# A two-layer hybrid attention backbone on one core: shared weights in the output projection, and other orders of projections

## The chip, the cores and the metric

The kernel runs on one core of one Trainium2 chip. The metric is the device time of one execution in microseconds; the time shown for a kernel is the median of its runs. A profiled execution of the same kernel gives the trace, whose times count from the first instruction of the program.

## The reference: what is computed

512 latent tokens and 256 context tokens, all of width 1024, pass two layers in float32. In each layer the rows are RMS-normalised and modulated (scale and shift from a conditioning vector), and one wide input projection feeds three token mixers: multi-head latent attention (MLA), differential attention, and windowed attention with sinks. Each mixer's output is gated by a SiLU path and projected; the three are merged by sigmoid gates and go through one output projection, whose result is gated and added to the rows. Only layer 0 also updates the context tokens.

```python
h_lat = rms_norm(x, norm_g) * (1.0 + scale) + shift
h_ctx = rms_norm(ctx, norm_g) * (1.0 + scale_c) + shift_c
...
terms.append(jax.nn.sigmoid(gr) * ((y * jax.nn.silu(zr)) @ w_branch[r]))
return (terms[0] + terms[1] + terms[2]) @ w_out
...
x = x + gate * merge_branches((ya_l, yb_l, yc_l), z_l, gm_l, w_branch, w_out)
if need_ctx:
    ctx = ctx + gate_c * merge_branches((ya_c, yb_c, yc_c), z_c, gm_c, w_branch, w_out)
```

The last step is an RMS norm of the latent tokens.

## The kernel before, in words

**Tokens and passes.** The 768 tokens are six tiles of 128: tiles 0 and 1 are context, 2 to 5 latent. A float32 product is made of three matmuls on rounded operands: every activation and every weight is split into a high part (rounded by ACT) and a low part (the rest, subtracted by DVE), and the passes are high-high, high-low and low-high. So one contraction block of 128 costs three matmuls. Projections produce feature-major results with the weights as the stationary operand; the output projection produces token-major results with the tokens as the stationary operand and the weights moving, up to 512 columns wide.

**Weights.** All weights come through one stream (`weight_stream`, L392). An item is 128x1024 numbers, 512 KB: `loader` (L397) issues its load on SP into one of two staging buffers (`ws`), and `splitter` (L409) makes its high and low halves in a ring of six buffers (`wh`), so three items are split at a time. A buffer comes free when the last matmul that reads it is done.

**The order of the work.** A planner (`Plan`, L128 on) writes the program: it keeps a modelled time for PE and for every other engine, and emits an instruction when its modelled inputs are ready. What it emits is in order on each engine; on the chip the engines then wait for each other through semaphores. PE is fed from three sources, chosen in `run` (L195): single pieces that became ready (transposes, the modulation's matmuls) go first; stream a holds the attention units in the order windowed, differential, MLA; stream b holds everything else as a list of entries in order (`stream_b`, L1209), at most `DEPTH` = 2 of them in flight, and serves as filler between softmax chains. An entry waits until its slots (46 buffers of 128x768), its gate and its first weight item are ready. The order of stream b is written by hand in two tables. `SEQ` (L45) orders the first projections of each layer: `K` and `Q` and `V` are keys, queries and values of windowed attention, `k`, `q`, `v` of the differential one, `c`, `cn`, `cr` and `p` MLA's queries (latent, norm, rotated part, plain part), `l`, `ln`, `lr`, `u`, `w` its keys and values, and `z20` to `z15` gate projections done early. `BR` (L30) orders the gate projections (`z`), merge gates (`g`) and branch projections (`b`) of the three branches, windowed first. A gate projection waits for all of its mixer's outputs. The constants of the planner's model are in `dma_t` (L334), `score` (L785) and `mod_entry` (L1621).

**The output projection** stands at the end of a layer. `load_res` (L1777) loads the residual rows and the gate vectors. `out_entry` (L1800) makes one block of columns for a set of token tiles: per contraction block it issues three matmuls per tile, and after the eighth it evicts (`chain`): DVE multiplies by the gate and adds the rows, ACT squares for the next norm. The block that ends at column 1024 is the final one: there, for layer 0, a latent tile's new rows are stored to DRAM (`x1_d`, L1850) for layer 1's residual, and `norm_rows` (L661) scales the rows in place, which has to wait until the store has read them. In layer 0 the latent tiles run three blocks (512, 256 and 256 columns) over eight weight items, and then the context tiles two blocks of 512 over the same weights, loaded and split again as eight more items. Between the two stands `next_h` (L1866), which allocates layer 1's inputs and starts `make_group` (L711): it transposes the normalised rows on PE (`make_h`, L671) once all four latent tiles are normalised, modulates each feature block on ACT or DVE and splits it. Layer 1's first projections need these blocks one after the other.

```python
        wide_ = [(0, 512), (512, 512)]
        for c, (a, n) in enumerate([(0, 512), (512, 256), (768, 256)]):
            out_entry(range(2, 6), 0, c, a, n, not cx)
        if cx:
            entry(next_h, need=16)
            for c, (a, n) in enumerate(wide_):
                out_entry(range(2), 1, c, a, n, True)
```

PSUM has four single banks (`bk`) and two double ones (`wd`); the latent tiles' sums and the context's lie in `bk`, the transposes' results in `wd`.

Of the kernel before, what the change touches and what calls it, by code (L numbers as in the profile page):

```python
# [24 lines left out]
D = 1024  # L25
# [4 lines left out]
BR = [['z7 z1 z2 g4 z4 z0 z3 g3 z5 z6 g0 b0 g1 b1 g2 b2 b4 g5 b5 b3 g6 b6 g7 b7', 'z7 z5 z0 z1 z6 z2 z3 g0 z4 g1 g2 g3 b3 b1 g4 b2 b0 b4 g5 g6 b5 g7 b6 b7', 'z7 z2 z6 z3 z1 z5 z4 g0 z0 g2 g1 g3 g4 g5 b1 g6 g7 b0 b3 b2 b4 b5 b6 b7'], ['g0 z4 z3 z0 z5 z7 z2 z1 z6 b0 g1 g5 b1 g2 b2 g3 g4 b3 b4 g6 g7 b6 b5 b7', 'z0 z5 z2 z1 g2 z4 z6 z7 g0 g1 z3 b0 g4 b1 g3 b4 g5 b5 b3 g6 b6 b2 g7 b7', 'z1 z4 z0 z2 z5 g0 z7 z6 g2 z3 g1 g5 g3 g4 g6 g7 b1 b2 b3 b4 b5 b0 b6 b7']]  # L30
# [14 lines left out]
SEQ = ["K0 V Q0 Q1 c0 c1 c2 cn Q2 cr p0 p1 Q3 p2 p3 z20 Q4 K1 z21 Q5 z22 Q6 z23 Q7 v0 k0 q0 z24 k1 q1 v1 k2 q2 l0 l1 ln lr k3 q3 v2 k4 q4 k5 q5 v3 k6 q6 k7 q7 u0 w0 z10 z11 u1 w1 z12 z13 u2 w2 z14 z15 u3 w3",  # L45
       "K0 V Q0 Q1 c0 c1 c2 cn Q2 cr p0 p1 Q3 p2 p3 z20 Q4 K1 z21 Q5 z22 Q6 z23 Q7 v0 k0 q0 z24 k1 q1 v1 k2 q2 l0 l1 ln lr k3 q3 v2 k4 q4 k5 q5 v3 k6 q6 k7 q7 u0 w0 z10 z11 u1 w1 z12 z13 u2 w2 z14 z15 u3 w3"]
# [189 lines left out]
def hybrid_kernel(tc, x_in, c_in, ctx_in, c_ctx, w_mod, b_mod, norm_g, w_in, q_norm, w_uq, kv_norm, w_ukv,  # L236
# [97 lines left out]
    def dma_t(nbytes):  # L334
        P.free["Q"] = max(P.free["Q"], P.now) + 620.0
        t = max(P.free["D"], P.free["Q"] + 650.0) + nbytes / 350.0
        P.free["D"] = t
        return t + 1050.0
# [446 lines left out]
    def score(row, kgroups, maps):  # L785
# [9 lines left out]
        P.tick(0.0 if maps == 1 else 300.0)  # L795
# [491 lines left out]
    def build_layer(o):  # L1287
# [333 lines left out]
        def mod_entry(ll, n, j):  # L1621
            def h():
# [7 lines left out]
                def chain():  # L1630
# [5 lines left out]
                    te = yield from P.pe(lambda: max(t, bk.gate() if j == 0 else 0.0), 750.0, emit)  # L1636
# [140 lines left out]
        def load_res(toks, j):  # L1777
# [3 lines left out]
            def chain():  # L1781
# [5 lines left out]
                G[j] = yield from tmps(2)  # L1787
                for h in range(2):
                    t = max(t, dma(G[j][h][0], gate_d[l][j, h * 512:(h + 1) * 512].partition_broadcast(128)))
# [4 lines left out]
                o.rest[j].t = t  # L1794
# [3 lines left out]
        o.rest = [When(), When()]  # L1798

        def out_entry(toks, j, c, a0, n, last):  # L1800
# [5 lines left out]
            if final and j == 0:  # L1806
                steps = [(tk, k) for tk in toks for k in range(8)]

            def release():
                yield o.rest[j]  # L1810
                for _, rg in G[j]:
                    rg.t = P.now + 3000.0
# [144 lines left out]
```

## Time and profile before

| | us |
|---|---|
| median of 3 runs (lowest to highest) | 2715.02 (2711.09 to 2715.76) |
| the profiled execution's own time | 2711.5 |
| its span, first to last instruction | 2709.7 |
| PE busy | 2632.3 |
| DVE busy | 1615.4 |
| ACT busy | 1350.7 |

The profiled execution's span and its time differ by what lies around the program. A busy PE is not PE at its peak: matmuls are pipelined, so the mean duration of a single one is longer than its share of the time, and a price per matmul is the busy time of a dense group over its count. The granted clock of TensorE has two levels, 1.2 and 2.4 GHz; the column PEclk is their mean over a stretch, as a share of the higher.

### The profile page before, as it was taken

Reading aid. Unit: us, or ns where it says so; the run is one execution under the profiler, and the core shown is the slowest. Engines: PE = TensorE matmul, PEld = TensorE weight load, DVE = VectorE, ACT = ScalarE, POOL = GpSimd, SP = SyncE. Lnnn points to the kernel's source line nnn. Section 1 sums busy time; section 2 is a strip of 40 time slices with the busy share of each in tenths; the row PEclk is TensorE's granted clock in tenths of the full one; section 3 lists DMA queues with packets and bytes.
Section 4 is the critical chain, followed back from the end, with each engine's and each line's share of the span. In section 5 each row is a group of like instructions: output and inputs, shape, how many; then the busy total and the mean of one; then the engine's idle time right before and its main releaser. Section 6 shows DMA issues by size and latency. Waiting matters only on the chain. (4 is left out here: it accounts for less than half of the span.)

```text
span 2709.7 us, 42486 instructions
## 1 busy us (share of the span) xinstructions
PE 2632.3 (97%) x16551; PEld 2291.5 (85%) x16551; DVE 1615.4 (60%) x3010; ACT 1350.7 (50%) x2685; POOL 179.3 (7%) x371
## 2 busy tenths in 40 slices
PE   7999999999999999999999998999999999999998
PEld 5888898888888888888888887898888788888887
DVE  4677887666676652142424577887667676534435
ACT  5676775545665551121222366777546565422333
POOL 2101111111100000000000011111101100000000
PEclk8999999999999999999999999999999999999999
DMA  7133211111132463442322533312111223443433
GB/s 237 47 96 85 66 43 48 53 51 42 49 85 85 140 201 117 121 133 63 103 69 64 186 97 91 85 51 65 55 50 38 72 75 98 122 140 101 131 94 133
DMA packets 332318, 249.55 MB, mean 92 GB/s; under 512 B 24870, under 2 KB 296324, under 8 KB 332116
## 3 DMA queue, kind: packets, MB, share of 16 engines
q1 hardware_dynamic: 331472, 246.50, 31.2%
q8 instruction: 130, 2.13, 0.3%
q0 software_dynamic: 416, 0.30, 0.1%
q14 instruction: 72, 0.59, 0.1%
q10 hardware_dynamic: 228, 0.03, 0.0%
HBM read 211.37 MB, written 35.41 MB: 91 GB/s over the span
## 5 line engine op out<-in xcount | busy, mean ns | idle before, releaser
L444 PE MATMUL wd<-s,wh 128*128 128x512 f32 (+1 forms) x4392 | 852.2, 355 | 2.0 <-DVE s L330 1.5
L444 PEld LDWEIGHTS wd<-s,wh 128*128 128x128 f32 x4392 | 723.7, 189 | 123.1 <-issue 6.7
L444 PE MATMUL bk<-s,wh 128*128 128x512 f32 (+1 forms) x3666 | 763.4, 355 | 8.0 <-DVE s L323 1.8
L444 PEld LDWEIGHTS bk<-s,wh 128*128 128x128 f32 x3666 | 584.2, 190 | 94.9 <-issue 6.8
L323 DVE TENSOR_TENSOR wh<-ws,wh 128x1024 fp32r<-128x1024 f32 (+4 forms) x294 | 324.3, 1108 | 522.5 <-ACT wh L309 520.2
L309 ACT ACTIVATE wh<-ws 128x1024 fp32r<-128x1024 f32 (+4 forms) x294 | 282.9, 967 | 537.7 <-PE wd L444 396.4
L309 ACT ACTIVATE pt<-bk 128x512 fp32r<-128x512 f32 (+3 forms) x604 | 342.2, 583 | 204.8 <-PE bk L914 143.3
L444 PE MATMUL bk<-wh,s 128*128 128x256 f32 (+1 forms) x2400 | 351.3, 300 | 3.9 <-DVE pt L323 3.0
L444 PEld LDWEIGHTS bk<-wh,s 128*128 128x128 f32 x2400 | 319.0, 192 | 19.8 <-DVE pt L323 3.7
L323 DVE TENSOR_TENSOR pt<-bk,pt 128x512 fp32r<-128x512 f32 (+5 forms) x428 | 273.3, 656 | 89.7 <-ACT pt L309 69.8
L444 PE MATMUL bk<-pt,s 128*128 128x256 f32 x1888 | 282.7, 289 | 16.2 <-DVE pt L323 10.6
L444 PEld LDWEIGHTS bk<-pt,s 128*128 128x128 f32 x1888 | 252.5, 192 | 41.0 <-DVE pt L323 19.4
L444 PE MATMUL wd<-s,s 128*128 128x256 f32 (+5 forms) x1872 | 274.3, 332 | 10.2 <-ACT s L309 7.4
L309 ACT ACTIVATE s<-wd,ti 128x768 f32<-128x768 f32 (+1 forms) x240 | 195.3, 817 | 137.7 <-DVE ti L826 79.8
L444 PEld LDWEIGHTS wd<-s,s 64*128 64x128 f32 (+2 forms) x1872 | 210.3, 190 | 38.8 <-ACT s L309 11.9
L914 PE MATMUL bk<-ident,s 128*128 128x128 f32 x1472 | 213.0, 278 | 7.9 <-DVE ti L866 3.0
L914 PEld LDWEIGHTS bk<-ident,s 128*128 128x128 f32 x1472 | 173.3, 143 | 34.5 <-ACT s L309 6.1
L309 ACT ACTIVATE s<-s,ti 128x513 f32<-128x513 f32 (+6 forms) x256 | 183.1, 722 | 26.6 <-DVE ti L862 11.0
L309 ACT ACTIVATE s<-bk 128x256 fp32r<-128x256 f32 (+5 forms) x291 | 113.1, 424 | 77.8 <-PE bk L444 76.5
L826 DVE TENSOR_REDUCE ti<-wd 128x1 f32<-128x768 f32 (+1 forms) x160 | 129.3, 845 | 26.0 <-PE wd L444 25.7
L309 ACT ACTIVATE yo<-bk 128x256 f32<-128x256 f32 (+1 forms) x200 | 72.2, 382 | 141.3 <-PE bk L444 140.1
L862 DVE CUSTOM_DVE_ANT_0 s<-wd,s,sinkt 128x512 f32<-128x512 f32 (+2 forms) x160 | 116.3, 743 | 42.1 <-PE wd L444 41.9
(104 smaller groups left out, 1557.1 us busy)
## 6 DMA issues: line engine op xcount, KB each, us to landing
ws<-in_w_in_dram SPq DMA_DIRECT2D x180, 512.0 KB
ws<-in_w_branch_dram SPq DMA_DIRECT2D x48, 512.0 KB
s<-in_w_mod_dram SPq DMA_DIRECT2D x48, 256.0 KB
s<-in_w_mod_dram SPq DMA_DIRECT2D x32, 384.0 KB
ws<-in_w_out_dram SPq DMA_DIRECT2D x24, 512.0 KB
y<-yo SPq DMA_DIRECT2D x80, 128.0 KB
s<-y SPq DMA_DIRECT2D x24, 384.0 KB
s<-s SPq DMA_DIRECT2D x22, 384.0 KB
```

The costliest lines, as they stand in the source:

```text
L309: lambda: nc.scalar.activation(out=out, in_=in_, func=func, scale=scale, **kw))
L323: t = yield from dve(ready, lambda: nc.vector.tensor_tensor(out=out, in0=a, in1=b, op=op), n)
L444: nc.tensor.matmul(o, lhsT=l, rhs=r, start=first, stop=last)
L826: t = yield from dve(t, lambda: nc.vector.tensor_reduce(out=nmx, in_=p[:, lo:hi], axis=AX.X, op=ALU.max, negate=True), n)
L862: t = yield from dve(t, lambda: nc.vector.tensor_tensor_reduce(out=pt_[:, 0:n], in0=p[:, lo:hi], in1=mk, scale=1.0, scalar=sk, op0=ALU.add ...
L914: nc.tensor.transpose(out=pp[:, j * 256 + ri2 * 128:j * 256 + ri2 * 128 + 128], in_=row["P"][:, c:c + 128], identity=ident)
```

## The change

In layer 0 the output projection takes all six token tiles through the same three column blocks (512, 256, 256), so each weight item is loaded and split once and used by all six. The context tiles' sums move into the two halves of a `wd` pair. `next_h` moves in the list from behind the latent tiles' last block to ahead of the last block, which in token order ends with the two context tiles. Residual rows and gates of all six tiles are loaded in one entry. `SEQ` and `BR` list the same entries in other orders, and four constants of the planner's model change. Layer 1 has no context update; its output projection stays as it was.

```diff
-BR = [['z7 z1 z2 g4 z4 z0 z3 g3 z5 z6 g0 b0 g1 b1 g2 b2 b4 g5 b5 b3 g6 b6 g7 b7', 'z7 z5 z0 z1 z6 z2 z3 g0 z4 g1 g2 g3 b3 b1 g4 b2 b0 b4 g5 g6 b5 g7 b6 b7', 'z7 z2 z6 z3 z1 z5 z4 g0 z0 g2 g1 g3 g4 g5 b1 g6 g7 b0 b3 b2 b4 b5 b6 b7'], ['g0 z4 z3 z0 z5 z7 z2 z1 z6 b0 g1 g5 b1 g2 b2 g3 g4 b3 b4 g6 g7 b6 b5 b7', 'z0 z5 z2 z1 g2 z4 z6 z7 g0 g1 z3 b0 g4 b1 g3 b4 g5 b5 b3 g6 b6 b2 g7 b7', 'z1 z4 z0 z2 z5 g0 z7 z6 g2 z3 g1 g5 g3 g4 g6 g7 b1 b2 b3 b4 b5 b0 b6 b7']]
+BR = [["z7 z4 z2 z1 g4 z0 g2 z3 g0 z5 z6 g3 b4 b2 b0 g1 b3 g6 b1 g5 b5 g7 b6 b7",
+       "z7 z0 z3 z5 z1 z6 z4 g1 g2 g0 z2 g3 b1 g5 b3 b2 g4 b4 g6 b5 b0 g7 b6 b7",
+       "z6 z7 z1 z2 z3 z0 z4 g5 g2 g1 g3 z5 g6 g0 g4 b1 b0 b4 g7 b3 b7 b2 b6 b5"],
+      ["z0 z3 g0 z7 z4 z5 z2 z6 g2 z1 g5 b0 b2 g1 g4 g3 b3 b1 b4 g6 g7 b6 b5 b7",
+       "z7 z0 z5 z2 g0 g2 z4 z1 z3 g1 z6 g4 b1 g3 b0 b4 g5 g6 b3 b5 b6 g7 b2 b7",
+       "z4 z0 z7 z1 z2 z6 g0 z3 z5 g2 g1 g3 g6 g4 g5 b1 b3 b2 b4 g7 b0 b5 b6 b7"]]
...
-SEQ = ["K0 V Q0 Q1 c0 c1 c2 cn Q2 cr p0 p1 Q3 p2 p3 z20 Q4 K1 z21 Q5 z22 Q6 z23 Q7 v0 k0 q0 z24 k1 q1 v1 k2 q2 l0 l1 ln lr k3 q3 v2 k4 q4 k5 q5 v3 k6 q6 k7 q7 u0 w0 z10 z11 u1 w1 z12 z13 u2 w2 z14 z15 u3 w3",
-       "K0 V Q0 Q1 c0 c1 c2 cn Q2 cr p0 p1 Q3 p2 p3 z20 Q4 K1 z21 Q5 z22 Q6 z23 Q7 v0 k0 q0 z24 k1 q1 v1 k2 q2 l0 l1 ln lr k3 q3 v2 k4 q4 k5 q5 v3 k6 q6 k7 q7 u0 w0 z10 z11 u1 w1 z12 z13 u2 w2 z14 z15 u3 w3"]
+SEQ = ["cn Q0 K0 V Q1 c0 c2 c1 Q2 Q3 cr p1 z20 p2 p0 p3 Q4 z21 K1 Q5 z22 Q6 z23 k1 Q7 v0 k0 v1 q0 z24 q1 k3 q2 k2 l0 v2 l1 ln lr q3 q5 k4 q4 k5 v3 k6 q6 u0 q7 k7 w0 z11 z10 u1 w1 z12 w2 z13 z14 u2 z15 u3 w3",
+       "K0 V cn Q0 Q1 c1 c0 c2 Q2 cr p0 p1 Q3 p2 p3 z20 Q4 K1 z21 Q5 z22 Q6 z23 Q7 v0 l0 k0 q0 k1 z24 v1 k2 q1 q2 q3 l1 lr k3 q4 v2 ln k4 k5 q5 v3 k6 q6 k7 q7 u0 z10 w0 z11 u1 z12 z13 u2 w2 w1 z15 z14 u3 w3"]
...
-        P.free["Q"] = max(P.free["Q"], P.now) + 620.0
-        t = max(P.free["D"], P.free["Q"] + 650.0) + nbytes / 350.0
+        P.free["Q"] = max(P.free["Q"], P.now) + 520.0
+        t = max(P.free["D"], P.free["Q"] + 650.0) + nbytes / 380.0
...
-        P.tick(0.0 if maps == 1 else 300.0)
+        P.tick(0.0 if maps == 1 else 385.0)
...
-                    te = yield from P.pe(lambda: max(t, bk.gate() if j == 0 else 0.0), 750.0, emit)
+                    te = yield from P.pe(lambda: max(t, bk.gate() if j == 0 else 0.0), 1200.0, emit)
...
-            if final and j == 0:
+            if final:
                 steps = [(tk, k) for tk in toks for k in range(8)]
...
-                    yield lambda: max(at(it_["ready"]), at(mt_[k]), bk.gate() if k == 0 else 0.0)
+                    yield lambda: max(at(it_["ready"]), at(mt_[k]), 0.0 if k > 0 or tk == 1 else bk.gate() if tk > 1 else wd.gate())
                     wv = v3(it_, kn, n)
-                    if k == 0:
+                    if k == 0 and tk > 1:
                         o_["ps"], o_["rel"] = bk.take()
+                    elif k == 0:
+                        if tk == 0:
+                            B["w"] = wd.take()
+                        o_["ps"], o_["rel"] = B["w"][0][:, 512 * tk:512 * tk + 512], B["w"][1] if tk else When()
...
-        entry(lambda: load_res(range(2, 6), 0), need=8, gate=lambda: max(w.t for w in mod_done[l][4:6]))
-        if cx:
-            entry(lambda: load_res(range(2), 1), need=4)
+        toks = (2, 3, 4, 5, 0, 1) if cx else (2, 3, 4, 5)
+        entry(lambda: load_res(toks, (0, 1) if cx else (0,)), need=2 * len(toks), gate=lambda: max(w.t for w in mod_done[l][4:6]))
         for tk in range(6):
             xd[tk] = When()
-        wide_ = [(0, 512), (512, 512)]
         for c, (a, n) in enumerate([(0, 512), (512, 256), (768, 256)]):
-            out_entry(range(2, 6), 0, c, a, n, not cx)
-        if cx:
-            entry(next_h, need=16)
-            for c, (a, n) in enumerate(wide_):
-                out_entry(range(2), 1, c, a, n, True)
+            if c == 2 and cx:
+                entry(next_h, need=16)
+            out_entry(toks, c, a, n)
```

## Rows read from the trace of the kernel before

**Rows 1.** The page, busy us (share of the span) and instructions of each engine.
```profile
PE 2632.3 (97%) x16551; PEld 2291.5 (85%) x16551; DVE 1615.4 (60%) x3010; ACT 1350.7 (50%) x2685; POOL 179.3 (7%) x371
```
**Rows 2.** Stretches: length, busy us of PE, PEld, DVE, ACT, POOL; clock, DMA share.
```profile
90.00:415.00 325.00, 312.32 (x2095) 284.09 (x2094) 249.53 (x609) 235.90 (x517) 38.17 (x105) 0.99 0.24 67
415.00:790.00 375.00, 370.02 (x2627) 322.57 (x2626) 259.60 (x497) 208.47 (x460) 43.34 (x82) 0.99 0.18 50
790.00:990.00 200.00, 193.40 (x1369) 169.84 (x1369) 135.75 (x252) 117.94 (x259) 2.24 (x5) 1.00 0.43 132
990.00:1495.00 505.00, 505.00 (x3011) 438.93 (x3010) 160.22 (x181) 112.75 (x137) 0.00 (x0) 1.00 0.35 103
1495.00:1570.00 75.00, 71.30 (x422) 63.19 (x422) 46.17 (x77) 33.38 (x59) 2.21 (x4) 1.00 0.52 168
1570.00:1860.00 290.00, 278.33 (x1750) 248.31 (x1749) 227.97 (x499) 207.98 (x428) 35.85 (x79) 0.99 0.29 79
1860.00:2175.00 315.00, 308.62 (x2137) 266.86 (x2136) 213.76 (x368) 176.61 (x354) 35.37 (x58) 0.99 0.20 53
2175.00:2335.00 160.00, 154.34 (x1001) 137.57 (x1000) 117.20 (x205) 97.40 (x197) 3.61 (x5) 0.99 0.35 102
2335.00:2690.00 355.00, 353.53 (x1631) 295.34 (x1630) 153.74 (x186) 107.61 (x145) 0.00 (x0) 1.00 0.41 119
```
**Rows 3.** The same view of three stretches of 50 us.
```profile
100.00:150.00 50.00, 48.41 (x321) 44.61 (x321) 31.76 (x86) 32.02 (x80) 2.99 (x10) 0.93 0.16 43
...
1500.00:1550.00 50.00, 46.30 (x299) 42.16 (x298) 26.09 (x50) 17.27 (x35) 2.21 (x4) 1.00 0.50 168
1550.00:1600.00 50.00, 50.00 (x322) 45.44 (x321) 38.51 (x70) 33.33 (x67) 2.40 (x3) 1.00 0.38 109
```
**Rows 4.** PE's waits, 90 to 415 and 1860 to 2335: us, times, longest.
```profile
PE bk L444 <- DVE pt L323: 4.0, 10, 0.8
...
PE wd L444 <- ACT s L309: 7.9, 5, 2.6
```
**Rows 5.** Groups of instructions, 1494.9 to 1569.2: busy us, mean ns | idle before.
```profile
L444 PE MATMUL bk<-wh,s 128*128 128x512 f32 x192 | 44.5, 391 | 0.0
L444 PE MATMUL bk<-wh,s 128*128 128x256 f32 x192 | 23.2, 283 | 0.0
L323 DVE TENSOR_TENSOR wh<-ws,wh 128x1024 fp32r<-128x1024 f32 x15 | 18.3, 1221 | 15.0 <-ACT wh L309 14.9
L309 ACT ACTIVATE wh<-ws 128x1024 fp32r<-128x1024 f32 x15 | 15.9, 1058 | 18.6 <-DMA ws<-in_w_out_dram 7.7 <-PE bk L444 3.4 <-PE wd L444 3.3
```
**Rows 6.** Timeline of PE, 1538 to 1576: start us, us [idle before].
```profile
1545.24 0.49 PE L682 MATMUL wd<-ident,s 128*128 128x128 f32 x3
1549.43 1.64 PE L682 MATMUL wd<-ident,s 128*128 128x128 f32 x13 [3.70 <-DVE s L665]
1550.83 2.32 PE L444 MATMUL bk<-wh,s 128*128 128x512 f32 x9
1552.99 1.91 PE L682 MATMUL wd<-ident,s 128*128 128x128 f32 x16
1554.65 14.57 PE L444 MATMUL bk<-wh,s 128*128 128x512 f32 x63
```
**Rows 7.** Timeline of all engines, 1528 to 1582: the last latent token, then the modulated inputs.
```profile
1542.18 0.41 DVE L323 TENSOR_TENSOR pt<-bk,pt 128x256 f32<-128x256 f32 x1
...
1544.04 0.42 DVE L323 TENSOR_TENSOR s<-s,pt 128x256 f32<-128x256 f32 x1
1544.18 0.94 SPq L341 DMA_DIRECT2D x1d<-s  x2
...
1548.89 1.05 DVE L665 TENSOR_SCALAR s<-s,ti 128x512 f32<-128x512 f32 x2 [3.46 <-DMA x1d<-s]
...
1551.00 0.81 DVE L703 TENSOR_SCALAR pt<-wd,modc 128x512 f32<-128x512 f32 x1
...
1562.42 0.68 DVE L323 TENSOR_TENSOR s<-pt,s 128x512 fp32r<-128x512 f32 x1
```

More of the change, by code (lines that the diff above doesn't have):

```diff
@@ L1775, in build_layer, with load_res @@
         s4 = {}
-        def load_res(toks, j):
+        def load_res(toks, js):
             for tk in toks:
@@ L1786, in chain @@
                         t = max(t, dma(X[tk][h][:, 0:512], src[:, h * 512:(h + 1) * 512]))
-                G[j] = yield from tmps(2)
-                for h in range(2):
-                    t = max(t, dma(G[j][h][0], gate_d[l][j, h * 512:(h + 1) * 512].partition_broadcast(128)))
+                for j in js:
+                    G[j] = yield from tmps(2)
+                    for h in range(2):
+                        t = max(t, dma(G[j][h][0], gate_d[l][j, h * 512:(h + 1) * 512].partition_broadcast(128)))
                 if l == 1:
@@ L1793, in chain @@
                         t = max(t, dma(o.fn[hh][0], final_norm[hh * 512:(hh + 1) * 512].partition_broadcast(128)))
-                o.rest[j].t = t
+                o.rest.t = t
             P.spawn(chain())
@@ L1797, in load_res, with out_entry @@
             yield
-        o.rest = [When(), When()]
-        def out_entry(toks, j, c, a0, n, last):
+        o.rest = When()
+        def out_entry(toks, c, a0, n):
             kn = 1024 // n
@@ L1805, in out_entry @@
             steps = [(tk, k) for i in range(8 // kn) for tk in toks for k in range(kn * i, kn * i + kn)]
-            if final and j == 0:
+            if final:
                 steps = [(tk, k) for tk in toks for k in range(8)]
             def release():
-                yield o.rest[j]
-                for _, rg in G[j]:
-                    rg.t = P.now + 3000.0
+                yield o.rest
+                for g in G.values():
+                    for _, rg in g:
+                        rg.t = P.now + 3000.0
             def o_h(*its):
@@ L1836, in chain @@
                         x = X[tk][h][:, cc:cc + n]
-                        yield o.rest[j]
-                        t = yield from tt(max(t, o.rest[j].t), y, o_["ps"][:, 0:n], G[j][h][0][:, cc:cc + n], ALU.mult)
+                        yield o.rest
+                        t = yield from tt(max(t, o.rest.t), y, o_["ps"][:, 0:n], G[0 if tk > 1 else 1][h][0][:, cc:cc + n], ALU.mult)
                         o_["rel"].t = t
@@ L1861, in o_h @@
                     P.spawn(release())
-                    if last:
-                        free(16, P.now)
+                    free(16, P.now)
             entry(o_h, its)
```

## The prediction

> **What bounds the kernel now.** I read the page's busy times first, then stretches of the span cut at the stages, then PE's waits, and last the seam between the two layers instruction by instruction. PE is busy for 97% of the span and DVE for 60% [rows 1]: the time is PE's work plus what PE loses. The stretches show where it loses [rows 2]. In the dense ones (990 to 1495, 2335 to 2690) PE idles for 0.0 and 1.5 us, so no order of entries can win anything there. What is left after the start-up, length less PE busy, lies in the attention stages, where projections run as filler between softmax chains: 12.7 us in 90 to 415 (windowed attention of layer 0), 5.0 in 415 to 790 (differential), 6.6 in 790 to 990 (latent), 11.7 in 1570 to 1860 (windowed, layer 1), 6.4 in 1860 to 2175 and 5.7 in 2175 to 2335. Beside the idle time stands the clock: 100 to 150 was granted 0.93 [rows 3], and since the clock has two levels (1.2 and 2.4 GHz) that is 0.07 x 50 = 3.5 us lost in one fall. The waits are short and many: the costliest group in the first attention stage is 4.0 us in 10 waits for DVE's low halves; in layer 1 the scores waited 7.9 us for exponentials, 2.6 at the longest [rows 4]. No single wait is a lever.
>
> At the seam (1495 to 1570) PE idles for 75.00 - 71.30 = 3.7 us, all of it in one gap ahead of the transposes for layer 1 [rows 2, 6].
>
> **The change, part by part.**
>
> *Shared weights.* Layer 0's output projection takes 8 weight items in place of 16: eight loads of 512 KB and eight pairs of splits go, 1.06 us of ACT and 1.22 us of DVE each [rows 5], 8.5 and 9.8 us of engine time. On PE's path that is worth nothing by itself: PE waited for none of these items, as the one gap of the stage is the transposes' [rows 6]. The cover was 12 or 24 matmuls per item (2.8 or 5.6 us at 232 ns) and becomes 36 (8.4 us). If the cover failed, the price would be a split pair, 2.3 us each; I take 0. The loads of the residual rows and gates are the same number on SP, now all ahead of the first quarter-pair; the first eviction needs them only after the first column block, 144 matmuls or 33 us long, so again 0.
>
> *Narrower columns for the context.* Its two tokens ran 96 matmuls of 512 columns; now they run 48 of 512 and 96 of 256. From the groups of this stage [rows 5]: 44.5/192 = 232 ns and 23.2/192 = 121 ns. So 48 x 232 = 11.1 us become 96 x 121 = 11.6 us: **+0.5 us**, all on PE. The Trainium skill (TensorE: Matmul & The Clock Gate, Back-to-back issue gap) gives a warm matmul N/2.4 + 2.5 ns, by which halving N would cost about 0.1 us here, an estimate; the rows show a larger fixed part, and the sum goes by the rows.
>
> *The seam.* This is the part that speaks against the change. Latent matmuls end at 1545.24 - 24 x 0.232 = 1539.7 [rows 6]. The last latent token is then multiplied by its gate at 1542.18 and added at 1544.04, its store goes out at 1544.18 to 1545.12, and the normalisation, which overwrites the row, waits for that store until 1548.89 [rows 7]. Transposes go on at 1549.43: 9.7 us after the last latent matmul. 24 context matmuls covered 5.6 us of it; 3.7 us are the gap. Then the modulated, split inputs of layer 1 come one feature block at a time; the last low half starts at 1562.42 and takes 0.68, so it stands 13.7 us after 1549.43 [rows 7]. The other 72 context matmuls (16.7 us, [rows 6]) cover all of it.
>
> After the change only the context's last quarter lies behind the last latent token: 48 x 121 ns = 5.8 us. The transposes' entry stands ahead of that quarter in the list, but its pieces wait for the normalised rows, so this moves nothing by itself. Ahead of the transposes I bound the gap by the chain as it was, 9.7 - 5.8 = 3.9 us, and by the chain without what stood in its way. In the way were splits of weights on DVE and two weight loads on SP ahead of the last store; with shared items the next three items are split before the last quarter ends. Then the chain is 0.41 + 0.42 for the eviction, about 0.4 of hand-over, 1548.89 - 1545.12 = 3.8 for the store, 1.05 for two normalisations and 0.3 of hand-over, 6.4 us, and the gap 0.6 us. Behind the transposes nothing of layer 0 is left. PE has the 32 transposes (3.6 us), the latent half of the first projection (24 x 232 ns = 5.6 us) and, because two entries may be in flight, one token of the value projection (2.9 us), each paced by the feature blocks. Upper bound: the 13.7 us stay, plus 0.7 us for the last block's matmuls, and values do not run ahead: 14.4 - 3.6 - 5.6 = 5.2 us idle. Lower: nothing but the wait for the first block, taken as 1.6 us from the first modulation at 1551.0 (its 0.81 and one split pair, less the transposes beside them). The whole seam then idles between 0.6 + 1.6 = 2.2 us and 3.9 + 5.2 = 9.1 us, against 3.7 now. I take 4.7, below the middle, because fewer splits compete on DVE: **+1.0 us**, ends -1.5 and +5.4. What is late next, if the store is not, are these feature blocks, which DVE and ACT make at about 1 us each.
>
> *The other orders.* All entries remain, so PE's work is unchanged; only the fillers' neighbours change, and the planner's four constants only move where it puts them. Layer 0's projections are reordered from the start (the fourth query block ahead of the rotated part, a gate projection between the narrow MLA projections, which carry much eviction per matmul). Layer 1's list keeps its order up to its last query block but for one entry that issues nothing while it waits, so the 11.7 us of 1570 to 1860 stay. The hand-over from differential to latent attention stays too: in both orders the next branch begins with gate projections that wait for all of that attention. What the order can reach is 12.7 + 6.6 + 5.7 = 25.0 us of idle time [rows 2] and falls of the clock at 3.5 us. No row prices an order. The ends are +8 us (a third of that again, should the new neighbours be worse) and -16 us (two thirds gone); I take a third gone, **-8.3 us**, since the groups that spread heavy evictions concern the first stage above all, and most single waits there are under 1 us.
>
> *Sum.* 0.5 + 1.0 - 8.3 = -6.8 us. The profiled execution took 2711.5 us (its span 2709.7), which puts it at 2704.7; but it lies at the low end of the three runs, whose median is 2715.0. Against that median the forecast is 2715.0 - 6.8 = **2708 us**.
>
> **The rivals.** A measurement of this kernel can tell about 0.2%, 5.4 us, from no change.
>
> *Order gives nothing.* The waits are set by the attention chains' ACT and DVE work, and moving fillers shifts them from one unit to the next. For it: DVE is busy 250 of 325 us in the first stage, 228 of 290 in layer 1's [rows 2], whatever the order. Against it: PE idles in some units and not in others of the same kind. Time: 2715.0 + 0.5 + 1.0 = 2716.5 us. Chance 0.30.
>
> *The seam opens (slower).* Place: from the end of the context's last quarter to the first projection of layer 1. Price: the upper end, 9.1 us idle against 3.7, plus 0.5: 2715.0 + 5.9 = 2720.9 us with no gain from the order. It decides, against a neutral order, once the seam idles for more than 3.7 + 5.4 - 0.5 = 8.6 us. For it: 72 covering matmuls disappear. Against it: the waits on splits and loads shrink too. Chance 0.20. In 0.05 of cases, counted inside these, the clock falls as well: +3.5 us, 2724 us. The gap of 3.7 us passed without a fall, both stretches around it being granted 1.00 [rows 3]. The same page of the Trainium skill (Why this matters for your kernels) warns that idle gaps between bursts of matmuls bring the half clock back; this seam does not bear that out so far.
>
> *The new neighbours are worse.* +8 us: 2715.0 + 1.5 + 8 = 2724.5 us. Chance 0.06.
>
> *The named move doesn't happen.* If the transposes do come ahead of part of the context's quarter, those matmuls cover the feature blocks instead of the normalisation, and the seam's sum is the same; 2708 us either way, so it has no share of its own.
>
> **How the numbers follow.** The forecast, a gain from the order with the seam about even, has 0.44, and its own times run from 2695 to 2709.6 us. Faster by over 0.2% is this case: 0.44. Within 0.2%: 0.30, the neutral order. Slower: 0.20 + 0.06 = 0.26. For 8 in 10 the range reaches to 2695 below (2715.0 + 1.5 - 16 = 2700 with a seam at its better end and one fall of the clock less, 3.5 us, leaves about 0.08 out) and to 2724 above (the opened seam with a fall of the clock), which leaves about 0.1 out.
>
> **What would show it.** Eight fewer loads of the output weights, 48 fewer 512-column matmuls and 96 more of 256; PE's idle time between the last latent matmul and layer 1's first projection at 2 to 9 us, 4.7 by my choice, ended by the normalisation first and by the low halves second; PE's idle time in 90 to 415 and in latent attention down by a third while layer 1's windowed attention stays near 11.7 us. The prediction is wrong if the attention stages keep their idle sums, if the seam idles for over 8.6 us, or if new falls of the clock appear.

## The result and the profile after

The changed kernel takes **2684.6 us** (median of 4 runs, 2680.6 to 2686.8) against 2713.9 for the kernel before, measured beside it (2711.1 to 2715.8): a ratio of 0.9891, 95% interval 0.9874 to 0.9908, or 29 us less. The forecast was 2708 and the range began at 2695: the sign was right, the size was not.

The page of the changed kernel, as [rows 1], with the span, the line of memory traffic and the one of the output weights' loads. Its lines of code stand 5 below those of before (L444 is now L449, L323 L328).

```profile
span 2682.8 us, 42573 instructions
PE 2624.9 (98%) x16599; PEld 2290.8 (85%) x16599; DVE 1607.9 (60%) x3009; ACT 1340.3 (50%) x2678; POOL 172.2 (6%) x371
HBM read 207.17 MB, written 35.41 MB: 90 GB/s over the span
ws<-in_w_out_dram SPq DMA_DIRECT2D x16, 512.0 KB
```

The change did what it says: 16599 - 16551 = 48 more matmuls, 16 loads of the output weights in place of 24, and 4.2 MB less read (211.37 before), which is eight loads of 512 KB. The profiled execution took 2684.55 us, 27 less than the profiled one of before. Of its span's 26.9 us, 19.5 are idle time of PE (span less PE busy: 77.4 before, 57.9 now) and 7.4 are busy time.

The same stretches as [rows 2], cut at the corresponding points of the work, the start-up first (with other orders, a stretch does not hold quite the same entries): length, busy us of PE, PEld, DVE, ACT, POOL; clock, DMA share.

```profile
0.00:80.00 80.00, 67.34 (x392) 47.67 (x393) 40.60 (x109) 44.99 (x115) 15.57 (x33) 0.91 0.64 209
...
80.00:413.00 333.00, 324.23 (x2229) 298.52 (x2228) 253.10 (x613) 235.91 (x525) 33.78 (x101) 0.99 0.25 68
413.00:775.00 362.00, 357.35 (x2510) 309.17 (x2508) 253.65 (x490) 205.05 (x451) 44.73 (x82) 0.99 0.18 50
775.00:970.00 195.00, 188.85 (x1339) 167.02 (x1340) 134.72 (x257) 117.03 (x261) 1.93 (x5) 1.00 0.42 123
970.00:1484.50 514.50, 514.50 (x3074) 446.55 (x3074) 165.20 (x187) 115.83 (x140) 0.00 (x0) 1.00 0.36 107
1484.50:1562.00 77.50, 73.97 (x469) 67.22 (x467) 38.20 (x72) 24.05 (x51) 2.76 (x5) 0.98 0.40 132
1562.00:1843.00 281.00, 274.09 (x1751) 245.59 (x1750) 223.44 (x490) 205.42 (x424) 30.63 (x77) 0.99 0.28 74
1843.00:2157.00 314.00, 308.81 (x2131) 266.61 (x2130) 219.22 (x376) 182.08 (x362) 38.26 (x60) 0.99 0.20 54
2157.00:2304.00 147.00, 146.51 (x989) 132.39 (x988) 111.81 (x198) 94.27 (x194) 2.30 (x5) 1.00 0.35 101
2304.00:2663.00 359.00, 359.00 (x1650) 299.97 (x1650) 158.78 (x193) 109.84 (x147) 0.00 (x0) 1.00 0.42 122
```

Length less PE busy, stage by stage, before against after:

| stage | idle before, us | after |
|---|---|---|
| start-up (0 to 90 before) | 14.8 | 12.7 |
| windowed, layer 0 | 12.7 | 8.8 |
| differential, layer 0 | 5.0 | 4.6 |
| latent, layer 0 | 6.6 | 6.1 |
| seam | 3.7 | 3.5 |
| windowed, layer 1 | 11.7 | 6.9 |
| differential, layer 1 | 6.4 | 5.2 |
| latent, layer 1 | 5.7 | 0.5 |
| dense end | 1.5 | 0.0 |

The three stages that the forecast let the order reach gave 25.0 - 15.4 = 9.6 us, near the 8.3 forecast. What it held fixed gave the rest of the idle time: 4.8 us in layer 1's windowed attention, some 5 in the start-up, the two differential stages and the dense end. The busy time fell with the clock. Six of the stretches of 50 us between 100 and 2650 were granted less than 1.00, three of them here:

```profile
100.00:150.00 50.00, 49.62 (x331) 45.74 (x332) 30.97 (x81) 29.26 (x72) 6.10 (x19) 0.97 0.17 40
550.00:600.00 50.00, 49.93 (x286) 43.08 (x285) 23.10 (x35) 19.43 (x35) 3.90 (x3) 0.93 0.27 70
1550.00:1600.00 50.00, 47.76 (x319) 44.05 (x318) 33.85 (x72) 30.77 (x65) 5.22 (x5) 0.97 0.29 83
```

One at 0.93 and five at 0.97 lose (0.07 + 5 x 0.03) x 50 = 11 us; the kernel before had two and six, 16 us. The 5 us between them are most of the 7.4 us of busy time. A second profiled execution of the changed kernel lost 7.5 us by the same sum (five at 0.97), so some 3.5 us of this can differ from one execution to the next.

**The seam.** PE's timeline in the changed kernel, as [rows 6]: start us, us [idle before, and what ended it].

```profile
1514.37 2.20 PE L449 MATMUL wd<-wh,s 128*128 128x512 f32 x9
1517.35 0.97 PE L449 MATMUL wd<-wh,s 128*128 128x512 f32 x3 [0.78 <-DVE pt L328]
...
1535.02 1.33 PE L449 MATMUL wd<-wh,s 128*128 128x256 f32 x9 [0.52 <-DVE pt L328]
1536.19 11.68 PE L449 MATMUL bk<-wh,s 128*128 128x256 f32 x96
1547.71 3.40 PE L449 MATMUL wd<-wh,s 128*128 128x256 f32 x27
1553.28 1.80 PE L449 MATMUL wd<-wh,s 128*128 128x256 f32 x12 [2.17 <-DVE pt L328]
1554.88 1.91 PE L687 MATMUL wd<-ident,s 128*128 128x128 f32 x8
```

All of the seam's idle time, 0.78 + 0.52 + 2.17 = 3.5 us, lies inside the context tiles' matmuls, one wait in each of the three column blocks, and none of it ahead of the transposes (L687). In the last block 24 matmuls of the first context tile and 3 of the second are done, and the second's other 21 wait for DVE. The same moment on all engines, as [rows 7]:

```profile
1552.41 0.49 DVE L670 TENSOR_SCALAR s<-s,ti 128x512 f32<-128x512 f32 x1 [0.73 <-POOL ti L663]
1552.81 0.42 DVE L328 TENSOR_TENSOR pt<-wd,pt 128x256 f32<-128x256 f32 x1
...
1553.28 1.80 PE L449 MATMUL wd<-wh,s 128*128 128x256 f32 x12 [2.17 <-DVE pt L328]
```

What PE waits for is the first tile's eviction (`pt<-wd`, done at 1553.23). The second tile's sum lies in the other half of the same `wd` pair, so it needs nothing from that eviction: it is a false wait, because the two halves count as one tile (the last experiment gives each its own). DVE is late since the eviction stands in order behind a latent row's normalisation, which itself waited 0.73 us for POOL. The wait came with a fall of the clock (0.97 in 1550 to 1600, above; 1.00 before [rows 3]), and again in the second execution (2.21 us of wait, 0.97).

### The profile page after: what moved, and what is told of

It is laid out like the page before. It is cut to its first block, busy times and chain, and to the rows that moved or that the text cites. A ratio compares the mean times of both kernels' runs of the same rounds, so it can differ in the third digit from the quotient of the medians.

```text
span 2682.8 us, 42573 instructions
## 1 busy us (share of the span) xinstructions
PE 2624.9 (98%) x16599; PEld 2290.8 (85%) x16599; DVE 1607.9 (60%) x3009; ACT 1340.3 (50%) x2678; POOL 172.2 (6%) x371
## 5 line engine op out<-in xcount | busy, mean ns | idle before, releaser
L449 PE MATMUL wd<-s,wh 128*128 128x512 f32 (+1 forms) x4392 | 850.9, 355 | 1.5 <-DVE s L335 0.7
L449 PEld LDWEIGHTS wd<-s,wh 128*128 128x128 f32 x4392 | 723.7, 189 | 121.8 <-issue 6.3
L449 PE MATMUL bk<-s,wh 128*128 128x512 f32 (+1 forms) x3666 | 769.5, 357 | 10.0 <-DVE pt L328 8.3
L449 PEld LDWEIGHTS bk<-s,wh 128*128 128x128 f32 x3666 | 586.7, 191 | 98.6 <-DVE pt L328 12.4
L328 DVE TENSOR_TENSOR wh<-ws,wh 128x1024 fp32r<-128x1024 f32 (+4 forms) x286 | 316.3, 1110 | 540.0 <-ACT wh L314 536.2
L314 ACT ACTIVATE wh<-ws 128x1024 fp32r<-128x1024 f32 (+4 forms) x286 | 274.4, 964 | 548.1 <-PE wd L449 419.6
L449 PE MATMUL bk<-wh,s 128*128 128x256 f32 (+1 forms) x2304 | 331.3, 295 | 1.0 <-DVE pt L328 0.4
L328 DVE TENSOR_TENSOR pt<-bk,pt 128x512 fp32r<-128x512 f32 (+4 forms) x424 | 270.6, 654 | 79.6 <-ACT pt L314 61.1
L449 PEld LDWEIGHTS bk<-wh,s 128*128 128x128 f32 x2304 | 300.0, 191 | 11.7 <-DVE pt L328 1.1
L449 PE MATMUL bk<-pt,s 128*128 128x256 f32 x1888 | 278.6, 287 | 7.8 <-DVE pt L328 5.8
L449 PEld LDWEIGHTS bk<-pt,s 128*128 128x128 f32 x1888 | 252.7, 191 | 30.3 <-DVE pt L328 13.4
L449 PE MATMUL wd<-s,s 128*128 128x256 f32 (+5 forms) x1872 | 271.2, 329 | 2.5 <-ACT s L314 2.3
L449 PEld LDWEIGHTS wd<-s,s 64*128 64x128 f32 (+2 forms) x1872 | 210.0, 188 | 31.4 <-issue 7.7
```

Source lines behind the costliest of these rows:

```text
L314: lambda: nc.scalar.activation(out=out, in_=in_, func=func, scale=scale, **kw))
L328: t = yield from dve(ready, lambda: nc.vector.tensor_tensor(out=out, in0=a, in1=b, op=op), n)
L449: nc.tensor.matmul(o, lhsT=l, rhs=r, start=first, stop=last)
```

## The experiments

Every ratio is against the kernel before, measured beside it on the same chip; its median there was between 2712.5 and 2716.0 us, so a difference in us between two runs from different chips can be off by about 3 us. "Tables" are `SEQ` and `BR`. Four parts can be put in or left out: the output projection, `SEQ`, `BR`, and the planner's constants. In the diffs of tables, `before` and `after` stand for the tables of the two kernels, and `before[1]` for the second string (layer 1's) of one.

### The parts alone

*Only the shared output projection, in the kernel before.*

```diff
+        toks = (2, 3, 4, 5, 0, 1) if cx else (2, 3, 4, 5)
...
         for c, (a, n) in enumerate([(0, 512), (512, 256), (768, 256)]):
+            if c == 2 and cx:
+                entry(next_h, need=16)
+            out_entry(toks, c, a, n)
...
```

> The kernel before with the shared output projection alone (old tables, old constants). Parts theory (each part of the change has its own price, and they add): the seam costs 1.5 to 3 us, all else stays, so 2714 + 2 = 2716 us, between 2714 and 2718. Draw theory (any change reshuffles the planner's whole program, and the time is drawn anew): anywhere from 2695 to 2730, with idle sums that change in stages which this edit does not touch, ahead of the seam above all.

Measured: 2714.4 us, beside 2714.4 before: ratio 1.0001 [0.9992, 1.0010].

*Only the tables.*

```diff
-SEQ, BR = before
+SEQ, BR = after
```

> The kernel before with the new tables alone (old output projection, old constants). Parts theory with the orders as the cause: nearly the whole gain and the seam's price back, 2714 - 31 = 2683 us, between 2678 and 2690. Constants theory (the planner's new constants place the entries better): 2705 to 2714. Draw theory: anything from 2690 to 2725, no part of the gain guaranteed.

Measured: 2704.4 us, 0.9963 [0.9948, 0.9978]. That is far from the first theory's 2683 and just under the second's range.

*Only the four constants.*

```diff
-        P.free["Q"] = max(P.free["Q"], P.now) + 620.0
-        t = max(P.free["D"], P.free["Q"] + 650.0) + nbytes / 350.0
+        P.free["Q"] = max(P.free["Q"], P.now) + 520.0
+        t = max(P.free["D"], P.free["Q"] + 650.0) + nbytes / 380.0
...
-        P.tick(0.0 if maps == 1 else 300.0)
+        P.tick(0.0 if maps == 1 else 385.0)
...
-  750.0, emit)
+  1200.0, emit)
```

> The kernel before with the planner's four new constants alone. Parts theory with the orders as the cause: 2711 to 2717 us. Constants theory: 2690 to 2700. Draw theory: anything from 2695 to 2730.

Measured: 2716.5 us, 1.0009 [0.9999, 1.0019].

*The changed kernel with the old output projection* (tables and constants together).

```diff
-            out_entry(toks, c, a, n)
+            out_entry(range(2, 6), 0, c, a, n, not cx)
```

> The changed kernel with the old output projection (context tiles behind, over their own weights), new tables and constants kept. Parts theory: the seam's price comes back, 2684.6 - 2.5 = 2682 us, between 2679 and 2685. Theory that sharing the weights itself brings the gain: 2705 or more. Draw theory: 2680 to 2710, with changed idle sums in layer 0 too.

Measured: 2684.6 us, 0.9890 [0.9875, 0.9904].

The projection is worth nothing that these runs can tell: put in alone it changes nothing within 3 us, taken out of the changed kernel nothing within 5. The 29 us are tables and constants **together**: on this chip -10.0 us by the tables alone and +2.1 by the constants alone would add up to -8, and the two together give -29.9.

### Which constant, with the new tables

*Tables and the two transfer constants.*

```diff
-        P.free["Q"] = max(P.free["Q"], P.now) + 620.0
-        t = max(P.free["D"], P.free["Q"] + 650.0) + nbytes / 350.0
+        P.free["Q"] = max(P.free["Q"], P.now) + 520.0
+        t = max(P.free["D"], P.free["Q"] + 650.0) + nbytes / 380.0
```

> The new tables with the old output projection and, of the planner's constants, only the two of the transfers new (520 ns and 380 bytes per ns). Between the tables alone (2704) and tables with all four constants (2684.6). If the transfers' constants make the tables fit: 2684 to 2690 us, with layer 1's windowed stage 6 us faster than with the tables alone. If the other two do: 2700 to 2706 us.

Measured: 2688.5 us, 0.9901 [0.9886, 0.9917].

*Tables and the cost of a differential score.*

```diff
-        P.tick(0.0 if maps == 1 else 300.0)
+        P.tick(0.0 if maps == 1 else 385.0)
```

> The new tables with the old output projection and, of the planner's constants, only the time booked per row of differential scores new (385 ns for 300). If this one makes the tables fit: 2690 us or less, with the gain in the differential stages alone (4 to 8 us over the two layers). If the transfers' constants do: 2697 to 2704 us. A draw would put it anywhere from 2690 to 2715.

Measured: 2695.6 us, 0.9931 [0.9917, 0.9946].

Against the tables alone the transfer constants bring 15.9 us, the score's 8.8, and all four 19.8, so they don't add; the 8.8 is no more than a schedule's luck is worth (below). The fourth was not tried alone. Where the transfer constants act is seen in layer 1's windowed attention. That stage with the tables alone, and then with the transfer constants added (columns as in [rows 2]):

```profile
1562.00:1858.00 296.00, 284.42 (x1770) 253.63 (x1769) 226.48 (x491) 204.80 (x419) 31.98 (x76) 0.98 0.30 79
```

```profile
1554.00:1840.00 286.00, 278.96 (x1789) 250.54 (x1788) 227.66 (x500) 209.76 (x432) 30.81 (x78) 0.99 0.30 81
```

PE idles for 11.6 us in the first and 7.0 in the second. PE's timeline in the first shows where. Filler are the matmuls `bk<-s,wh`, the only ones here with a weight operand:

```profile
1660.41 1.55 PE L449 MATMUL bk<-s,wh 128*128 128x512 f32 x6
1663.04 1.47 PE L919 MATMUL bk<-ident,s 128*128 128x128 f32 x10 [1.08 <-DVE s L328]
...
1669.16 0.74 PE L449 MATMUL wd<-s,s 128*128 128x256 f32 x4 [0.76 <-DVE ti L867]
1670.30 0.74 PE L449 MATMUL wd<-s,s 128*128 128x256 f32 x4 [0.40 <-DVE ti L867]
1671.72 0.45 PE L919 MATMUL bk<-ident,s 128*128 128x128 f32 x1 [0.69 <-DVE ti L871]
...
1674.19 2.04 PE L449 MATMUL bk<-s,wh 128*128 128x512 f32 x6
```

With the transfer constants, at the same point of the work:

```profile
1656.96 0.86 PE L449 MATMUL bk<-s,wh 128*128 128x512 f32 x3
1657.66 1.10 PE L449 MATMUL wd<-s,s 128*128 128x256 f32 x8
1658.60 2.91 PE L449 MATMUL bk<-s,wh 128*128 128x512 f32 x12
1661.36 1.03 PE L919 MATMUL bk<-ident,s 128*128 128x128 f32 x8
1662.14 2.30 PE L449 MATMUL bk<-s,wh 128*128 128x512 f32 x9
```

From 1662 to 1674 the first kernel has no filler between its attention pieces, and piece after piece waits for DVE; the second has filler between them. With the score's constant instead, the hole is the same and the stage idles for 11.5 us. The planner emits filler only when it believes the next weights to be loaded. That its slower model of a load held the filler back here is argued from the code; that these two numbers alone remove the hole, with the same tables, is measured. It may still be the luck of one schedule: a rate lower by one unit brings as much idle time back to this stage (below).

### Which table, with the new constants

*The changed kernel with the old `SEQ`.*

```diff
-SEQ = after
+SEQ = before
```

> The changed kernel with the old SEQ table (first projections), all else kept. If SEQ carries the gain that the tables and constants make together: 2704 to 2716 us, with the idle time of both windowed stages back. If BR carries it: 2684 to 2691 us. If neither does alone and the three were found together: 2692 to 2710 us.

Measured: 2711.3 us, 0.9993 [0.9983, 1.0002].

*The changed kernel with the old `BR`.*

```diff
-BR = after
+BR = before
```

> The changed kernel with the old BR table (gates and branch projections), all else kept. If BR carries the gain: 2704 to 2716 us, lost in the differential and MLA stages of both layers. If SEQ carries it: 2684 to 2691 us. If the three were found together: 2692 to 2710 us.

Measured: 2688.8 us, 0.9905 [0.9890, 0.9921].

Without the new `SEQ` nearly all is lost, 26.7 us. `BR` is worth 4 us at most, as its interval overlaps with the changed kernel's. Then `SEQ` by layer, always with the new `BR`, constants and projection:

*Layer 1's list as before* (layer 0's new).

```diff
-SEQ = [after[0], after[1]]
+SEQ = [after[0], before[1]]
```

> The changed kernel with layer 1's old list of first projections; layer 0's stays new. If each layer's list gains in its own layer: the 10 to 13 us of layer 0 stay, layer 1's 13 go, 2697 us, between 2693 and 2702. If layer 0's list alone carries it: 2684 to 2690. Draw: 2690 to 2712, with layer 0's stages no different from the changed kernel's in any case, as the program is the same there.

Measured: 2694.7 us, 0.9922 [0.9908, 0.9937].

*Layer 0's list as before* (layer 1's new).

```diff
-SEQ = [after[0], after[1]]
+SEQ = [before[0], after[1]]
```

> The changed kernel with layer 0's old list; layer 1's stays new. If each layer's list gains in its own layer: 2711 - 13 = 2698 us, between 2694 and 2703. If layer 0's list alone carries it: 2708 to 2713. If layer 1's alone: 2685 to 2690.

Measured: 2704.1 us, 0.9959 [0.9944, 0.9974]. This lies outside all three ranges: layer 1's list gives less than expected.

*Both as before, but for the end of layer 1's list.*

```diff
-u0 w0 z10 z11 u1 w1 z12 z13 u2 w2 z14 z15 u3 w3
+u0 z10 w0 z11 u1 z12 z13 u2 w2 w1 z15 z14 u3 w3
```

> Both lists old but for the end of layer 1's, from the first MLA keys on, where gate projections now stand between the MLA keys and values that need four slots each. Base is the kernel with both lists old, 2711.3 us. Slot theory (the old end leaves PE without filler when differential attention ends, since keys and values wait for slots): 5 to 6 us come from there, 2704 to 2707 us, and PE's waits of scores for exponentials there fall from about 4 us to 1. Rival (the end gains only with the rest of the list): 2709 to 2713 us.

Measured: 2702.4 us, 0.9954 [0.9937, 0.9971].

*Both as before, but for the front of layer 0's list.*

```diff
-K0 V Q0 Q1 c0 c1 c2 cn Q2 cr p0 p1 Q3 p2 p3 z20 Q4 K1 z21 Q5 z22 Q6 z23 Q7
+cn Q0 K0 V Q1 c0 c2 c1 Q2 Q3 cr p1 z20 p2 p0 p3 Q4 z21 K1 Q5 z22 Q6 z23 Q7
```

> Both lists old but for the front of layer 0's, up to its last windowed query block: queries first, the fourth query block ahead of the rotated part, a gate projection between the narrow MLA projections. Base is the kernel with both lists old, 2711.3 us. Spreading theory (neighbours with little eviction let DVE and ACT catch up): 4 to 6 us gained ahead of 300 us, 2705 to 2708 us. Rival (the gain there comes from the differential projections pulled forward, which are not in this front): 0 to 2 us, 2709 to 2712 us.

Measured: 2706.7 us, 0.9969 [0.9959, 0.9980].

From the old `SEQ`'s 2711.3 us, layer 0's list brings 16.6 us and layer 1's 7.2, 23.8 of the 26.7. Layer 1's part is all in its end, 14 entries of gate projections and latent keys and values: with that end alone it is 8.9 us. The front of layer 0's list is 4.6 of its 16.6, no more than luck can make (below).

The list and the idle time do not keep to their layers. Layer 1's windowed attention with layer 1's new list and layer 0's old one (seq1):

```profile
1577.00:1860.00 283.00, 271.81 (x1758) 243.87 (x1757) 223.13 (x493) 207.67 (x428) 29.67 (x76) 1.00 0.28 73
```

It idles for 11.2 us, against 6.9 in the changed kernel, though its own list is the same.

What the end of layer 1's list does is seen at the end of its differential attention. PE's waits from 2100 to 2160 (us in total, times, longest), the stretch itself, and PE's timeline, with the old `SEQ`:

```profile
PE wd L449 <- ACT s L314: 3.8, 2, 2.6
```

```profile
2100.00:2160.00 60.00, 55.74 (x347) 47.21 (x347) 41.88 (x74) 36.65 (x74) 8.27 (x13) 0.94 0.22 57
```

```profile
2132.59 2.37 PE L449 MATMUL bk<-s,wh 128*128 128x512 f32 x12
2137.52 0.58 PE L449 MATMUL wd<-s,s 64*128 64x256 f32 x1 [2.56 <-ACT s L314]
2139.35 2.29 PE L449 MATMUL wd<-s,s 64*128 64x256 f32 x11 [1.25 <-ACT s L314]
```

The same three with the new end of the list:

```profile
PE wd L449 <- ACT s L314: 0.5, 1, 0.5
```

```profile
2100.00:2160.00 60.00, 56.42 (x355) 46.65 (x355) 41.37 (x75) 37.39 (x75) 8.37 (x13) 1.00 0.25 68
```

```profile
2133.72 5.79 PE L449 MATMUL bk<-s,wh 128*128 128x512 f32 x27
...
2140.45 1.30 PE L449 MATMUL wd<-s,s 64*128 64x256 f32 x11 [0.50 <-ACT s L314]
```

Where the scores wait for exponentials, 12 matmuls of filler stood and now 27 do: the wait of 3.8 us is 0.5. Other waits take most of it back (the stretch's idle time goes from 4.3 to 3.6 us only), but the clock, 0.94 there, stays at 1.00, which is 0.06 x 60 = 3.6 us more. So the waits cost about as much by the clock as by their length. The other half of the gain lies in the latent attention behind, first with the old `SEQ`, then with the new end:

```profile
2160.00:2350.00 190.00, 184.89 (x1201) 162.91 (x1200) 134.35 (x235) 114.98 (x230) 2.97 (x8) 1.00 0.34 98
2160.00:2350.00 190.00, 189.31 (x1231) 167.94 (x1228) 140.55 (x241) 116.13 (x233) 3.35 (x8) 1.00 0.35 99
```

Its idle time falls from 5.1 to 0.7 us. Together 0.7 + 3.6 + 4.4 = 8.7 us, close to the 8.9 measured. This is not the luck of one schedule, as it shows in every profile: the seven kernels with the old end (the kernel before among them) are all granted 0.93 or 0.97 in 2100 to 2150 and idle for 4.2 to 5.7 us from 2170 to 2340; the eleven with the new end are all granted 1.00 in the first and idle for 0.5 to 3.7 us in the second, the most with the old `BR`.

### How much is the luck of one schedule

Three kernels move one constant of the planner by one unit; no instruction's work changes by it, only where the planner puts some.

*The changed kernel, with the tolerance of the planner's readiness tests 1 ns smaller (125 to 124).*

```diff
-TOPE = 125.0
+TOPE = 124.0
```

> The changed kernel with one planner constant off by 1 ns (the margin TOPE, 125 to 124), which reorders most of PE's program and is no change of any estimate. Fit theory (the new constants and tables together describe the chip better, so any program planned from them is good): 2681 to 2690 us. Draw theory (the tables were found for one exact program, and another one is a draw): 2692 to 2715 us, with idle time and falls of the clock back in the attention stages.

Measured: 2690.1 us, 0.9912 [0.9897, 0.9927].

*The changed kernel, with a transfer modelled a little slower.*

```diff
-        t = max(P.free["D"], P.free["Q"] + 650.0) + nbytes / 380.0
+        t = max(P.free["D"], P.free["Q"] + 650.0) + nbytes / 379.0
```

> The changed kernel with the planner's transfer rate at 379 in place of 380 bytes per ns, some 4 ns per weight item. Fit theory: 2681 to 2690 us. Draw theory: 2690 to 2715 us, nearer to the changed kernel than the other nudge, as fewer rows of PE's program differ.

Measured: 2692.4 us, 0.9924 [0.9909, 0.9939].

*The kernel before, with the first of these.*

```diff
-TOPE = 125.0
+TOPE = 124.0
```

> The kernel before with the same nudge, TOPE 125 to 124. Fit theory: the old tables and constants are a poorer description, 2711 to 2720 us. Draw theory: another draw, 2710 to 2735 us if the old tables too were found for one exact program, with no stage keeping its idle sum.

Measured: 2711.7 us, 0.9999 [0.9989, 1.0008].

The changed kernel loses 5.5 and 7.8 us by a nudge (the first loss is not clear of the noise, as the intervals overlap); the kernel before loses nothing by its one. The first result lies between the two theories, the second in the draw's range. The traces put most of the first loss into layer 0's windowed attention and most of the second into layer 1's. That stage at 379 bytes per ns, and a gap that the changed kernel does not have there:

```profile
1566.00:1853.00 287.00, 275.91 (x1762) 247.25 (x1761) 223.87 (x495) 207.95 (x428) 29.64 (x76) 0.99 0.27 72
1723.15 3.29 PE L449 MATMUL bk<-s,wh 128*128 128x512 f32 x9 [2.58 <-DVE s L328]
```

It idles for 11.1 us again, with tables and constants that but for this one unit are the changed kernel's. So single differences of 5 to 8 us between orders are no finding by their size alone, and neither are the 4 to 5 us of this stage; 20 to 29 us against the kernel before is what all three versions of the change give.

### The seam's false wait

*The changed kernel, each context tile with a `wd` pair of its own.*

```diff
-                    yield lambda: max(at(it_["ready"]), at(mt_[k]), 0.0 if k > 0 or tk == 1 else bk.gate() if tk > 1 else wd.gate())
+                    yield lambda: max(at(it_["ready"]), at(mt_[k]), 0.0 if k > 0 else bk.gate() if tk > 1 else wd.gate())
...
-                        if tk == 0:
-                            B["w"] = wd.take()
-                        o_["ps"], o_["rel"] = B["w"][0][:, 512 * tk:512 * tk + 512], B["w"][1] if tk else When()
+                        w_, o_["rel"] = wd.take()
+                        o_["ps"] = w_[:, 0:512]
```

> The changed kernel with each context tile's sums in a double bank of its own in place of two halves of one. My reading of the seam: PE's three gaps there (0.78, 0.52 and 2.17 us) are waits of the second context tile's matmuls for the first tile's eviction from the other half, a dependency by tile that the data don't have. Then they go, 3.5 us, and with them the fall of the clock behind the last (1.7 us), and the wait ahead of the transposes returns in part, 0.6 to 3.9 us: 2681 to 2686 us, if the rest of the program stays. Rival (the wait is for the normalisation anyway and only shows under another name): the same idle sum in the seam, 3.5 us within 0.5, ended by the normalisation, 2684 to 2686 us. Draw theory: the program behind the seam changes, so the time may go up to 2700 us whatever the seam does.

Measured: 2681.8 us, 0.9887 [0.9871, 0.9904]. The seam's stretch, and the one whose clock fell:

```profile
1484.50:1562.00 77.50, 76.01 (x496) 69.34 (x496) 40.08 (x77) 26.27 (x56) 2.76 (x5) 1.00 0.45 146
1550.00:1600.00 50.00, 48.51 (x331) 44.41 (x330) 36.00 (x75) 32.92 (x68) 5.21 (x5) 1.00 0.30 85
```

and the only two gaps left on PE from 1484 to 1572:

```profile
1553.38 1.09 PE L687 MATMUL wd<-ident,s 128*128 128x128 f32 x8 [0.72 <-DVE pt L328]
...
1556.25 1.97 PE L687 MATMUL wd<-ident,s 128*128 128x128 f32 x16 [0.71 <-DVE pt L708]
```

The waits among the context tiles are gone, the seam idles for 1.5 us and the clock stays at 1.00. Its time overlaps with the changed kernel's, which was measured on another chip; so here are both on one chip:

> The changed kernel with a double bank for each context tile, once more, beside the changed kernel on the same chip: 2 to 4 us under it (its seam idled 4.3 us less at equal work, the rest of the program being nearly the same). Rival (the one look's difference was the spread between runs): within 1 us of it.

> The changed kernel itself, as the other side of that comparison: 2682 to 2688 us.

Measured: 2678.8 us (2678.6 to 2679.3), 0.9874 [0.9859, 0.9888], with two pairs; 2683.9 us (2680.5 to 2686.7), 0.9896 [0.9879, 0.9912], as changed. The runs don't overlap: 5.1 us less, the fastest of all kernels here. By its size alone it could be the luck of a schedule. The rows of the seam account for some 3.5 of the 5.1: the gaps that it removes are worth 3.5 - 1.5 = 2.0 us and the fall 0.03 x 50 = 1.5 us. The rest is not told apart from luck.

## Why the prediction was right or wrong

**Shared weights, 0 us: right.** PE waited for none of the items, before or after, which is the reason given. The two runs that isolate the whole output projection (this, the narrower columns and the seam, +1.5 us forecast together) give no change within 3 and 5 us, too coarse to tell 0 from 1.5.

**The seam, 0.5 + 1.0 us: about right in size, wrong in mechanism.** In the traces the seam takes 77.5 us against 75.0 for about the same work, 2.5 more: 0.5 are the narrower columns, -0.2 idle time (3.5 against 3.7), 1.5 the fall of the clock, and some 0.7 no row accounts for. The step that failed is "ended by the normalisation first and by the low halves second": neither ends any gap (all three end with the eviction `pt<-wd`), the normalisation is covered, and the low halves find value projections beside them. I had costed the two halves of one `wd` pair at nothing, without asking what a matmul into one half waits for when the other is evicted. The fall of the clock was in the text, with a chance of 0.05 and as part of a slower kernel, and came in a faster one.

**The other orders, -8.3 us: wrong by more than 20.** Tables and constants together gave 29.9 us with the old projection. This is the step that failed, in three of its sentences.
- "The four constants only move where it puts them" priced them at nothing, and alone they are worth nothing. With the new tables they bring 19.8 us. Their price can't be read from the old order, since it depends on the tables that they are planned with.
- "The 11.7 us of 1570 to 1860 stay", since the list there keeps its order (but for `cn`; `c0` and `c1` change places too): they became 6.9. The list there is indeed not what did it. It takes the new transfer constants (11.6 us without, 7.0 with them) and layer 0's new list (11.2 without it), and one unit of the transfer rate undoes it (11.1). So the idle time of a stage, which the forecast held fixed with its list, hangs on the plan ahead of it as well, and that it came out well here is at least partly luck.
- "The hand-over from differential to latent attention stays too": the end of layer 1's list is worth 8.9 us with the new constants: a fall of the clock avoided (3.6 us) where waits of 3.8 us became 0.5, and 4.4 us of idle time in latent attention. I looked at the branch's first entries and not at the last 14 of `SEQ`, which decide how much filler is left when the scores wait.

Where I did let the order reach, a third of 25.0 us came close by luck: 9.6 us of idle time, but as 3.9, 0.5 and 5.2, and the largest, in layer 1's latent attention, came mostly by the end of the list, ahead of the hand-over that was to stay. I counted no fall of the clock in the forecast itself; five microseconds fewer were lost. New falls were named as a sign of being wrong, and one came, at the seam.

**The rivals.** "Order gives nothing" falls: DVE's busy time per stage hardly changed (253 of 333 us against 250 of 325) and PE's idle time still fell. "The seam opens" falls: 3.5 us, where it would have decided at 8.6. The seam's lower bound, 2.2 us of idle time, was beaten by the version with two pairs, 1.5 us.

**Left open.** About half of the gain. Layer 0's new list brings 16.6 us. Of these some 4 to 5 appear in layer 1's windowed attention, whose own list is the same in both kernels, so they may be the luck of a schedule; for the rest the traces show single short waits gone in many places, and no run isolates the pulled-forward differential projections behind `Q7`. What the fourth constant does was not tried alone either.

## What to carry to other kernels

In a statically planned kernel such as this one, an order of filler and the planner's model of when that filler is ready are one thing: test them together, and price each attention stage by the filler that is left when its longest wait comes. Nudge a constant that should not matter before believing a few microseconds of such a gain. And two sums that are evicted at different times should not share one PSUM tile: here matmuls of the second waited for the eviction of the first.

## What the runs showed of the hardware

A gap's length alone did not tell whether the clock falls. Before, 3.70 us of idle time at the seam passed at 1.00 [rows 3, 6]; with the new tables and the old projection, 3.55 us at the same place came with 0.91 in 1530 to 1550. In the changed kernel 2.17 us inside the context tiles came with 0.97 in that stretch of 50 us. The same wait, 2.19 to 2.65 us long, came with a fall in nine more profiles (the second execution of the changed kernel and eight other kernels) and without one in one kernel, that with layer 0's old and layer 1's new list (seq1):

```profile
1568.79 1.69 PE L449 MATMUL wd<-wh,s 128*128 128x256 f32 x12 [2.19 <-DVE pt L328]
1550.00:1600.00 50.00, 46.25 (x360) 44.41 (x361) 32.79 (x77) 25.85 (x61) 5.60 (x7) 1.00 0.31 97
```

With 0.72 and 0.71 us (two pairs) it was 1.00, and with 0.84 and 0.71 us in their second execution. The Trainium skill (TensorE: Matmul & The Clock Gate, Why this matters for your kernels) warns that idle gaps between bursts of matmuls bring the half clock back; most of these gaps agree with that, the 3.70 us before and the 2.19 us here do not. At the end of layer 1's differential attention, gaps of 2.56 and 1.25 us with a single short matmul of 64 rows between them came with 0.94, and cost about as much again by the clock as by the idle time.
